# Attention values from plain fp32 weights, two key tiles in the two column halves of the PE array

## The chip, the cores and the metric

The kernel runs on one core of a Trainium2 chip. The metric is the device time of one execution in microseconds (us). The core has a tensor engine (PE, with its weight loads listed apart as PEld), a vector engine (DVE), a scalar engine (ACT), GpSimd (POOL) and a queue engine (SP) that starts most transfers. They run at the same time and wait for each other through semaphores. The kernel uses eight PSUM banks of 128 x 512 fp32 (tags mm 3, z 2, av, tr and hg 1 each).

## The reference

One layer of a decoder over 2048 tokens of width 1024: an input projection, two head groups side by side (an HGRN2 recurrence with 4 heads, a stick-breaking attention with 8 heads of width 64), an output projection, a dense SwiGLU feed-forward block and a gated per-layer embedding. The change lies in the attention:

```python
z = jnp.einsum('bthd,bshd->bhts', qb, kp).astype(jnp.float32) * scale
causal = jnp.arange(t1)[None, :] < jnp.arange(t0, t1)[:, None]
log_1mb = jnp.where(causal, -jax.nn.softplus(z), 0.0)
rem = lax.cumsum(log_1mb, axis=3, reverse=True) - log_1mb
a = jnp.where(causal, jnp.exp(jax.nn.log_sigmoid(z) + rem), 0.0)
outs.append(jnp.einsum('bhts,bshd->bthd', a.astype(v.dtype), vp))
```

For each query t the weight of key s is a sigmoid times the product of (1 - sigmoid) over the keys between them, and the last line sums the values with these weights. Everything is fp32.

## The kernel before

**Precision.** fp32 operands of the large products are split: `hi` is the value cast to the type fp32r, `lo` is what the cast left out, also in fp32r. A product is then the sum of two or three fp32r matmuls into one PSUM bank (`mm3`, lines 221 to 223: hi.hi, lo.hi, hi.lo). The HGRN group uses plain fp32 matmuls instead, some of them into a part of the array's columns (lines 503 and 514).

**Tiling of the attention.** The tokens are cut into four groups g of 512. For each query group, head and key group c up to g there is a chunk: 512 queries against 512 keys, 80 chunks in all, 32 of them on the diagonal (c = g). A chunk has four units, 320 in all. In the first half of a unit (`weights_of`) PE computes the scores of 128 queries against the chunk's keys into a bank "z" (line 388), ACT takes two sigmoids, DVE runs the product along the keys (line 409) and POOL multiplies to the weights `a`, 128 queries x 512 keys (line 413). Values need the keys on the partitions, so in `turn_of` PE transposes the `a` of all four query tiles for one key tile of 128 (line 421) into the one bank "tr". On the diagonal, key tile sb needs only the query tiles from sb on: 512, 384, 256 and 128 columns. ACT casts the turned weights to `ah` (line 424), DVE subtracts to `al` (line 426), and one unit later `values_of` adds two fp32r matmuls to the bank "av" (lines 437 and 438).

**The values.** The eviction of the v projection (`evict`, lines 323 to 332) writes each head's 64 columns twice, high part and rest side by side, 128 columns to DRAM (`v_s`). So the stationary tile `vt` of a unit is 128 keys x 128, and rows 0 to 63 of "av" gather the high part's sums, rows 64 to 127 the rest's. At the end of a head ACT copies the lower rows and DVE adds the two halves (lines 442 and 443).

**Order.** PE's order is the program's. The attention is a generator that yields twice per unit: after `weights_of` of unit i, and after `values_of` of an older unit followed by `turn_of` of unit i - 4 (LAG = 4). `weave` spreads these steps between the steps of the main stream: the input projections of the four groups first, then the output projections of groups 0 to 2, with the HGRN generators between them. Then follow the feed-forward block and the embedding, without attention. A scheduler orders the other engines' queues, each of which runs in order. The buffers around the change: one bank "tr", one bank "av", two each of `ah`, `al`, `kt` and `vt`, eight of `a`.

Of the kernel before, what the change touches and what calls it, by code (L numbers as in the profile page):

```python
# [8 lines left out]
F32 = mybir.dt.float32  # L9
F32R = mybir.dt.float32r  # L10
# [3 lines left out]
ALU = mybir.AluOpType  # L14

P = 128
# [3 lines left out]
GT = 512  # L20
NG = T // GT
TT = GT // P
HH = 4
SBH = 8
SBD = 64
# [59 lines left out]
def hybrid_block(  # L85
# [6 lines left out]
    nc = tc.nc  # L92
    ctx.enter_context(tc.manual_schedule(engines={mybir.EngineType.PE}))
    x, p, out = x[0], p[0, 0], out[0]
# [6 lines left out]
    def scratch(name, shape):  # L101
        return [dram.tile(list(shape), F32, tag=f"{name}{g}", name=f"{name}{g}") for g in range(NG)]

    q_s = scratch("q_s", (2, SBH, SBD, GT))
    k_s = scratch("k_s", (SBH, 2, SBD, GT))
    v_s = scratch("v_s", (GT, SBH, P))
    hq_s = scratch("hq_s", (HH, P, GT))
    hf_s = scratch("hf_s", (HH, P, GT))
    hv_s = scratch("hv_s", (GT, HH * P))
# [75 lines left out]
    def ev(dt=F32, name="ev", shape=(P, GT)):  # L185
        return fb.tile(list(shape), dt, tag="ev", name=name, bufs=12)
# [5 lines left out]
    att = side.enter_context(tc.tile_pool(name="att", bufs=2, side="right"))  # L192
# [35 lines left out]
    def dense(nk, w_in_cols, act, w_stationary):  # L228

        banks = [mm_bank() for _ in range(2)]  # L230
        for kk in range(0, nk, 2):
            w = weight(w_in_cols(kk))
            for i in range(2):
                for k in range(2):
                    a = act[kk + k]
                    first, last = kk + k == 0, kk + k == nk - 1
                    if w_stationary:
                        o = k * 256 + i * P
                        mm3(banks[i], [t[:, o:o + P] for t in w], a, first, last)
                    else:  # L240
                        mv = [t[:, k * 256:(k + 1) * 256] for t in w]
                        for j in range(2):
                            mm3(banks[i][:, j * 256:(j + 1) * 256], cut(a, 2 * i + j), mv, first and j == 0, last and j == 1)
                if i == 0 or kk < nk - 2:
                    yield None
        yield banks
# [58 lines left out]
    def in_proj(g, u, kinds):  # L305
        def cols(c):
            return lambda k: w_in[k * P:(k + 2) * P, c:c + 256]

        def evict(kind, half, i, b):
            j = 2 * half + i  # L310
            if kind in ("q", "k"):
                hi, lo = ev(F32R, "ea"), ev(F32R, "eb")
                nc.scalar.copy(hi, b)
                nc.vector.tensor_tensor(lo, b, hi.bitcast(F32), op=ALU.subtract)
                for n, s in enumerate((hi, lo)):
                    if kind == "q":
                        d = q_s[g][n, 2 * j:2 * j + 2]
                    else:
                        d = k_s[g][2 * j:2 * j + 2, n]
                    for hh in range(2):  # L320
                        nc.sync.dma_start(d[hh], s[hh * SBD:(hh + 1) * SBD, :].bitcast(F32))
            elif kind == "v":
                for n in range(2):
                    t = 2 * i + n
                    vv = ev(F32R, "vv").rearrange("p (h i d) -> p h i d", h=SBH // 2, i=2)
                    b3 = b[:, n * 256:(n + 1) * 256].rearrange("p (h d) -> p h d", d=SBD)
                    nc.scalar.copy(vv[:, :, 0, :], b3)
                    nc.vector.tensor_tensor(
                        vv[:, :, 1, :], b3, vv[:, :, 0, :].bitcast(F32), op=ALU.subtract)
                    nc.sync.dma_start(  # L330
                        v_s[g][t * P:(t + 1) * P, half * SBH // 2:(half + 1) * SBH // 2],
                        vv.rearrange("p h i d -> p h (i d)").bitcast(F32))
            elif kind == "hq":
                sg, e = ev(), ev()
                nc.scalar.activation(sg, b, AF.Sigmoid)
                nc.vector.tensor_tensor(e, b, sg, op=ALU.mult)
                nc.sync.dma_start(hq_s[g][j], e)
            elif kind == "hf":
                e = ev()
                nc.scalar.copy(e, b)  # L340
                nc.sync.dma_start(hf_s[g][j], e)
            elif kind == "hv":
                e = ev()
                nc.scalar.copy(e, b)
                d = hv_s[g][2 * i * P:2 * (i + 1) * P, half * 256:(half + 1) * 256]
                nc.sync.dma_start(d.rearrange("(t p) d -> p t d", p=P), e.rearrange("p (t d) -> p t d", t=2))
            else:
                sg, e = ev(), ev()
                nc.scalar.activation(sg, b, AF.Sigmoid)
                nc.vector.scalar_tensor_tensor(e, b, g_hg[:, j:j + 1], sg, op0=ALU.mult, op1=ALU.mult)  # L350
                nc.sync.dma_start(hg_s[g][j], e)

        for kind, c in kinds:
            for half in range(2):
                for banks in dense(ND, cols(c * 512 + half * 256), u, kind not in ("v", "hv")):
                    if banks is None:
                        yield
                for i, b in enumerate(banks):
                    evict(kind, half, i, b)
                yield  # L360


    def attention():
# [10 lines left out]
        def chunk_start(st, c):  # L374
            h = st["h"]
            kt = att.tile([P, GT], F32R, tag="kt", name="kt", bufs=2)
            nc.sync.dma_start(kt.bitcast(F32), k_s[c][h].rearrange("i d t -> (i d) t"))
            vt = att.tile([P, TT, P], F32R, tag="vt", name="vt", bufs=2)
            nc.sync.dma_start(vt.bitcast(F32), v_s[c][:, h, :].rearrange("(b s) d -> s b d", s=P))
            return {"st": st, "c": c, "k": kt, "v": vt, "a": []}  # L380

        def weights_of(ch, tb):
# [33 lines left out]
        def turn_of(ch, sb):  # L416
            diag = ch["c"] == ch["st"]["g"]
            t0 = sb if diag else 0
            tr = bank("tr")
            for tb in range(t0, TT):  # L420
                nc.tensor.transpose(tr[:, tb * P:(tb + 1) * P], ch["a"][tb][:, sb * P:(sb + 1) * P], ident)  # L421
            lo_c = t0 * P
            hi = att.tile([P, GT], F32R, tag="ah", name="ah")
            nc.scalar.copy(hi[:, lo_c:], tr[:, lo_c:])  # L424
            lo = att.tile([P, GT], F32R, tag="al", name="al")
            nc.vector.tensor_tensor(lo[:, lo_c:], tr[:, lo_c:], hi[:, lo_c:].bitcast(F32), op=ALU.subtract)  # L426
            return ch, sb, lo_c, hi, lo

        def values_of(ch, sb, lo_c, hi, lo):
            st, c = ch["st"], ch["c"]  # L430
            g = st["g"]
            first = c == g and sb == 0
            last = c == 0 and sb == TT - 1
            if first:
                st["av"] = bank("av")
            av = st["av"]
            nc.tensor.matmul(av[:, lo_c:], ch["v"][:, sb, :], hi[:, lo_c:], start=first, stop=False)
            nc.tensor.matmul(av[:, lo_c:], ch["v"][:, sb, :], lo[:, lo_c:], start=False, stop=last)
            if last:
                h = st["h"]  # L440
                o = att.tile([SBD, GT], F32, tag="avo", name="avo", bufs=1)
                nc.scalar.copy(o, av[SBD:P, :])
                nc.vector.tensor_tensor(o, av[0:SBD, :], o, op=ALU.add)
                nc.sync.dma_start(o_s[g][HH + h // 2][(h % 2) * SBD:(h % 2 + 1) * SBD, :], o)

        units, turned = [], []
        chunks = [(g, h, c) for g in range(NG) for h in range(SBH) for c in range(g, -1, -1)]
        n_units = len(chunks) * TT
        for i in range(n_units + LAG + 1):
            if i < n_units:  # L450
                if i % TT == 0:
                    g, h, c = chunks[i // TT]
                    if c == g:
                        st = head_start(g, h)
                    ch = chunk_start(st, c)
                weights_of(ch, i % TT)
                units.append((ch, i % TT))
            yield
            if turned:
                values_of(*turned.pop(0))  # L460
            if i >= LAG and i - LAG < n_units:
                turned.append(turn_of(*units[i - LAG]))
            yield

    LAG = 4

    def attention_steps(g):
        return SBH * (g + 1) * TT
# [657 lines left out]
    units = [attention_steps(g) for g in range(NG)]  # L1126
# [33 lines left out]
    turned = []  # L1160
# [5 lines left out]
    for g in range(NG - 1):  # L1166
        if g + 1 < NG - 1:
            out_load(g + 1, res[g + 1])
        op = Stream(out_proj(g, res[g]))
# [29 lines left out]
    op = Stream(out_proj(NG - 1, res[NG - 1]))  # L1199
# [73 lines left out]
```

## Time and profile before

| | |
|---|---|
| median of three runs | 3137.61 us (3127.91 to 3139.72) |
| the profiled execution's own time | 3140.98 us |
| its span, first to last instruction | 3139.2 us |
| mean granted TensorE clock | 0.971 |
| DVE, scan of the attention (line 409, 320 instructions) | 245.9 + 105.1 us |
| ACT, cast of the turned weights (line 424, 320 instructions) | 167.3 us, 523 ns each |
| POOL, the weights a (line 413, 320 instructions) | 314.0 us |

How to read the rows: a row of instructions has the line, the engine, the operation, out<-in, the shape, the count, the busy time with the mean of one in ns, and the idle time of that engine just before them with what ended it. A row of waits has who waited, for whom, the total in us, the times and the longest. A row of stretches has the window, its length, the busy time of each engine with its count, the granted clock and the share and rate of the transfers. A row of the timeline has the start, the length, the engine, the line, the operation and the count of merged instructions. Matmuls overlap, so what one costs is the time from its start to the next one's start.

### The profile page before, as it was taken

To read this page: it belongs to the slowest core of one execution; us is meant where nothing else is said; L and a number is where in the kernel's file an instruction comes from. 1 tells how busy PE (TensorE), PEld (TensorE's weight loads), DVE (VectorE), ACT (ScalarE), POOL (GpSimd) and SP (SyncE) were. 2 spreads that over 40 slices of the span, in tenths; PEclk is the share of its full clock that TensorE was granted. 3 is DMA by queue.
4 is the path that set the end of the run, shared out by engine and by line. 5 is a ranking of instruction groups with operands and counts; after the bars stand their busy time and mean duration, and the time that the engine had idled before them with its cause. 6 is when DMAs were issued, how large, how long until landed. Compare 5 with 4: busy or idle time off the path is not lost. (4 is left out here: it accounts for less than half of the span.)

```text
span 3139.2 us, 52948 instructions
## 1 busy us (share of the span) xinstructions
PE 2927.5 (93%) x18280; PEld 2455.3 (78%) x18280; DVE 2030.1 (65%) x2793; ACT 1587.0 (51%) x3187; POOL 1622.3 (52%) x1606
## 2 busy tenths in 40 slices
PE   7999899989999989778889999999999999998979
PEld 6888688868887878767767887888788888887757
DVE  3556566657677666654686677756786676746474
ACT  5666556656666666656543332355433333545432
POOL 3344355535556555755664444455744343657364
PEclk9999899989999999899999999999999999999989
DMA  6775465446445444546766676777855664678774
GB/s 189 224 212 163 128 182 162 146 134 174 150 142 156 145 138 118 182 134 228 239 219 208 228 246 220 225 230 221 290 185 186 204 217 132 220 221 278 253 258 148
DMA packets 463822, 607.02 MB, mean 193 GB/s; under 512 B 43456, under 2 KB 269760, under 8 KB 463552
## 3 DMA queue, kind: packets, MB, share of 16 engines
q1 hardware_dynamic: 463552, 603.63, 61.1%
q8 instruction: 144, 2.36, 0.3%
q14 instruction: 126, 1.03, 0.1%
HBM read 444.61 MB, written 158.86 MB: 192 GB/s over the span
## 5 line engine op out<-in xcount | busy, mean ns | idle before, releaser
L754 ACT CAST wh<-wr 128x512 fp32r<-128x512 f32 x600 | 354.1, 618 | 544.1 <-PE mm L222 165.6
L413 POOL TENSOR_TENSOR a<-be,ring 128x512 f32<-128x512 f32 (+2 forms) x320 | 314.0, 981 | 497.8 <-DVE ring L409 473.5
L755 POOL TENSOR_TENSOR wl<-wr,wh 128x512 fp32r<-128x512 f32 x256 | 370.4, 1454 | 360.9 <-ACT wh L754 343.6
L221 PE MATMUL mm<-uh,wh 128*128 128x512 f32 x1168 | 485.5, 416 | 4.4 <-DVE c L762 2.7
L223 PE MATMUL mm<-uh,wl 128*128 128x512 f32 x1168 | 461.8, 395 | 1.6 <-POOL wl L755 1.6
L222 PE MATMUL mm<-ul,wh 128*128 128x512 f32 x1168 | 461.2, 395 | 0.0
L755 DVE TENSOR_TENSOR wl<-wr,wh 128x512 fp32r<-128x512 f32 x344 | 313.0, 915 | 178.9 <-ACT wh L754 163.0
L221 PE MATMUL mm<-wh,uh 128*128 128x256 f32 (+1 forms) x1024 | 323.3, 316 | 9.0 <-ACT mix L643 6.4
L409 DVE TENSOR_TENSOR_SCAN ring<-z,ring,be 128x512 f32<-128x512 f32 x192 | 245.9, 1281 | 100.6 <-ACT z L395 96.9
L222 PE MATMUL mm<-wl,uh 128*128 128x256 f32 (+1 forms) x1024 | 306.7, 299 | 1.7 <-POOL wl L755 1.7
L223 PE MATMUL mm<-wh,ul 128*128 128x256 f32 (+1 forms) x1024 | 305.8, 299 | 0.0
L426 DVE TENSOR_TENSOR al<-tr,ah 128x512 fp32r<-128x512 f32 (+1 forms) x320 | 192.4, 601 | 113.3 <-ACT ah L424 112.6
L223 PEld LDWEIGHTS mm<-uh,wl 128*128 128x128 f32 x1168 | 222.2, 190 | 51.7 <-POOL wl L755 2.0
L221 PEld LDWEIGHTS mm<-uh,wh 128*128 128x128 f32 x1168 | 223.4, 191 | 46.9 <-DVE c L762 3.6
L207 ACT CAST wh<-wr 128x512 fp32r<-128x512 f32 x288 | 177.9, 618 | 151.9 <-PE mm L222 79.2
L222 PEld LDWEIGHTS mm<-ul,wh 128*128 128x128 f32 x1168 | 223.2, 191 | 38.6
L208 POOL TENSOR_TENSOR wl<-wr,wh 128x512 fp32r<-128x512 f32 x144 | 187.5, 1302 | 84.1 <-ACT wh L207 78.9
L394 ACT ACTIVATE be<-z 128x512 f32<-128x512 f32 (+2 forms) x320 | 170.9, 534 | 103.2 <-PE z L388 50.3
L221 PEld LDWEIGHTS mm<-wh,uh 128*128 128x128 f32 x1024 | 201.9, 197 | 17.8 <-ACT mix L643 7.2
L424 ACT CAST ah<-tr 128x512 fp32r<-128x512 f32 (+1 forms) x320 | 167.3, 523 | 95.6 <-PE tr L421 91.4
L222 PEld LDWEIGHTS mm<-wl,uh 128*128 128x128 f32 x1024 | 202.4, 198 | 7.3 <-POOL wl L755 2.0
L223 PEld LDWEIGHTS mm<-wh,ul 128*128 128x128 f32 x1024 | 201.9, 197 | 3.9
(287 smaller groups left out, 7256.5 us busy)
## 6 DMA issues: line engine op xcount, KB each, us to landing
wr<-in_w_gate_up_dram SPq DMA_DIRECT2D x308, 256.0 KB, 3.9
wr<-in_w_in_dram SPq DMA_DIRECT2D x224, 256.0 KB, 3.3
wr<-hid_s SPq DMA_DIRECT2D x154, 256.0 KB, 3.0
wr<-in_w_down_dram SPq DMA_DIRECT2D x110, 256.0 KB, 3.4
wr<-h_s SPq DMA_DIRECT2D x96, 256.0 KB, 4.3
hid_s<-hs SPq DMA_DIRECT2D x88, 256.0 KB, 3.1
wr<-wd_s SPq DMA_DIRECT2D x88, 256.0 KB, 3.5
kt<-k_s SPq DMA_DIRECT2D x80, 256.0 KB, 3.0
```

Source lines behind the costliest of these rows:

```text
L207: nc.scalar.copy(hi, src)
L208: (lo_engine or nc.gpsimd).tensor_tensor(lo, src, hi.bitcast(F32), op=ALU.subtract)
L221: nc.tensor.matmul(o, l[0], r[0], start=start, stop=False)
L222: nc.tensor.matmul(o, l[0], r[1], start=False, stop=False)
L223: nc.tensor.matmul(o, l[1], r[0], start=False, stop=stop)
L394: nc.scalar.activation(be[:, :n], z[:, :n], AF.Sigmoid, scale=0.125)
L409: nc.vector.tensor_tensor_scan(r[:, o:o + n][:, ::-1], z[:, :n][:, ::-1], be[:, :n][:, ::-1], init, op0=ALU.mult, op1=ALU.bypass)
L413: nc.gpsimd.tensor_tensor(a[:, :n], be[:, :n], r[:, o + 1:o + n + 1], op=ALU.mult)
L424: nc.scalar.copy(hi[:, lo_c:], tr[:, lo_c:])
L426: nc.vector.tensor_tensor(lo[:, lo_c:], tr[:, lo_c:], hi[:, lo_c:].bitcast(F32), op=ALU.subtract)
L754: nc.scalar.copy(hi, src)
L755: lo_engine.tensor_tensor(lo, src, hi.bitcast(F32), op=ALU.subtract)
```

## The change

One unit's values become one plain fp32 matmul. `v_s` holds each head's 64 columns once, and its eviction is one copy. `turn_of` makes one fp32 tile `at` by ACT's copy; DVE takes no part. `values_of` now runs once for two units: key tiles sb0 and sb0 + 1 each get one matmul with 64 stationary columns, the first into rows 0 to 63 of "av", the second into rows 64 to 127, that is, into the two column halves of the array. The sum of the two halves at the end of a head stays as it was. Since the first pair of a head has to start both halves on all 512 columns, key tile 1 of a diagonal chunk is filled up with zeros on its first 128 columns (POOL) and its matmul takes 512 columns instead of 384. `at` has three buffers. A pair runs in the second half of the step after its second tile was turned, so the first tile of a pair is used two units behind its turn, the second one unit.

```diff
-    v_s = scratch("v_s", (GT, SBH, P))
+    v_s = scratch("v_s", (GT, SBH, SBD))
...
-                    vv = ev(F32R, "vv").rearrange("p (h i d) -> p h i d", h=SBH // 2, i=2)
-                    b3 = b[:, n * 256:(n + 1) * 256].rearrange("p (h d) -> p h d", d=SBD)
-                    nc.scalar.copy(vv[:, :, 0, :], b3)
-                    nc.vector.tensor_tensor(
-                        vv[:, :, 1, :], b3, vv[:, :, 0, :].bitcast(F32), op=ALU.subtract)
+                    vv = ev(name="vv")[:, 0:256]
+                    nc.scalar.copy(vv, b[:, n * 256:(n + 1) * 256])
...
-            vt = att.tile([P, TT, P], F32R, tag="vt", name="vt", bufs=2)
-            nc.sync.dma_start(vt.bitcast(F32), v_s[c][:, h, :].rearrange("(b s) d -> s b d", s=P))
+            vt = att.tile([P, TT, SBD], F32, tag="vt", name="vt", bufs=2)
+            nc.sync.dma_start(vt, v_s[c][:, h, :].rearrange("(b s) d -> s b d", s=P))
...
-            hi = att.tile([P, GT], F32R, tag="ah", name="ah")
-            nc.scalar.copy(hi[:, lo_c:], tr[:, lo_c:])
-            lo = att.tile([P, GT], F32R, tag="al", name="al")
-            nc.vector.tensor_tensor(lo[:, lo_c:], tr[:, lo_c:], hi[:, lo_c:].bitcast(F32), op=ALU.subtract)
-            return ch, sb, lo_c, hi, lo
+            at = att.tile([P, GT], F32, tag="at", name="at", bufs=3)
+            nc.scalar.copy(at[:, lo_c:], tr[:, lo_c:])
+            if t0 == 1:
+                nc.gpsimd.memset(at[:, 0:lo_c], 0.0)
+                lo_c = 0
+            return lo_c, at
...
-            nc.tensor.matmul(av[:, lo_c:], ch["v"][:, sb, :], hi[:, lo_c:], start=first, stop=False)
-            nc.tensor.matmul(av[:, lo_c:], ch["v"][:, sb, :], lo[:, lo_c:], start=False, stop=last)
+            for i, (lo_c, at) in enumerate(pair):
+                nc.tensor.matmul(
+                    av[i * SBD:(i + 1) * SBD, lo_c:], ch["v"][:, sb0 + i, :], at[:, lo_c:], start=first, stop=last)
...
-            if turned:
-                values_of(*turned.pop(0))
+            if len(pair) == 2:
+                values_of(*units[i - LAG - 2], pair)
+                pair = []
             if i >= LAG and i - LAG < n_units:
-                turned.append(turn_of(*units[i - LAG]))
+                pair.append(turn_of(*units[i - LAG]))
```

Line numbers of the changed kernel are shifted by up to three: its scores stand on line 385, its transposes on 418, its copy on 421, its fill on 423 and its value matmuls on 437.

PE in the input projection of a later group, before: each unit has its two value matmuls ahead of its transposes.

```order
L437 MATMUL av<-ah,vt 128x512
L438 MATMUL av<-al,vt 128x512
L421 MATMUL tr<-ident,a 128x128 x3
L514 MATMUL hg<-qp,ks 32x32 x8
L221 MATMUL mm<-wh,uh 128x256
L222 MATMUL mm<-wl,uh 128x256
```

PE in the changed kernel, at a like place; the second transposes belong to the next unit.

```order
L437 MATMUL av<-at,vt 64x512 x2
L418 MATMUL tr<-ident,a 128x128 x4
L385 MATMUL z<-kt,q_9497 128x512
L385 MATMUL z<-kt,q_9500 128x512
L221 MATMUL mm<-uh,wh 128x512
L222 MATMUL mm<-ul,wh 128x512
L223 MATMUL mm<-uh,wl 128x512
L221 MATMUL mm<-uh,wh 128x512
L222 MATMUL mm<-ul,wh 128x512
L223 MATMUL mm<-uh,wl 128x512
L418 MATMUL tr<-ident,a 128x128 x3
```

Every second unit now has two narrow matmuls ahead of its transposes, and the other has none.

DVE in the first units of group 1, before (ring is the scan's output, ev and wl are other work of DVE):

```order
L336 TENSOR_TENSOR ev<-mm,ev 128x512
L409 SCALAR_TENSOR_TENSOR ring_251<-z,be 128x128
L426 TENSOR_TENSOR al<-tr,ah 128x512
L409 SCALAR_TENSOR_TENSOR ring_253<-z,be 128x256
L426 TENSOR_TENSOR al<-tr,ah 128x512
L409 SCALAR_TENSOR_TENSOR ring_255<-z,be 128x384
L208 TENSOR_TENSOR wl<-wr,wh 128x512
L426 TENSOR_TENSOR al<-tr,ah 128x512
L409 SCALAR_TENSOR_TENSOR ring_257<-z,be 128x512
L426 TENSOR_TENSOR al<-tr,ah 128x512
L409 SCALAR_TENSOR_TENSOR ring_251<-z,ring_251,be 128x512
L336 TENSOR_TENSOR ev<-mm,ev 128x512
```

The same place in the changed kernel:

```order
L333 TENSOR_TENSOR ev<-mm,ev 128x512
L406 SCALAR_TENSOR_TENSOR ring_251<-z,be 128x128
L406 SCALAR_TENSOR_TENSOR ring_253<-z,be 128x256
L406 SCALAR_TENSOR_TENSOR ring_255<-z,be 128x384
L208 TENSOR_TENSOR wl<-wr,wh 128x512
L406 SCALAR_TENSOR_TENSOR ring_257<-z,be 128x512
L406 SCALAR_TENSOR_TENSOR ring_251<-z,ring_251,be 128x512
L333 TENSOR_TENSOR ev<-mm,ev 128x512
```

The subtractions are gone, and the rest stands in the same order. On POOL each diagonal chunk has a fill between two products, here in group 0 of the changed kernel:

```order
L410 TENSOR_TENSOR a<-be,ring_257 128x512
L423 MEMSET at 128x128
L410 TENSOR_TENSOR a<-be,ring_251 128x128
L410 TENSOR_TENSOR a<-be,ring_253 128x256
L208 TENSOR_TENSOR wl<-wr,wh 128x512
```

Before, the rows there were the same without the fill.

More of the change, by code (lines that the diff above doesn't have):

```diff
@@ L324, in evict @@
                     t = 2 * i + n
-                    vv = ev(F32R, "vv").rearrange("p (h i d) -> p h i d", h=SBH // 2, i=2)
-                    b3 = b[:, n * 256:(n + 1) * 256].rearrange("p (h d) -> p h d", d=SBD)
-                    nc.scalar.copy(vv[:, :, 0, :], b3)
-                    nc.vector.tensor_tensor(
-                        vv[:, :, 1, :], b3, vv[:, :, 0, :].bitcast(F32), op=ALU.subtract)
+                    vv = ev(name="vv")[:, 0:256]
+                    nc.scalar.copy(vv, b[:, n * 256:(n + 1) * 256])
                     nc.sync.dma_start(
                         v_s[g][t * P:(t + 1) * P, half * SBH // 2:(half + 1) * SBH // 2],
-                        vv.rearrange("p h i d -> p h (i d)").bitcast(F32))
+                        vv.rearrange("p (h d) -> p h d", d=SBD))
             elif kind == "hq":
@@ L422, in turn_of, with values_of @@
             lo_c = t0 * P
-            hi = att.tile([P, GT], F32R, tag="ah", name="ah")
-            nc.scalar.copy(hi[:, lo_c:], tr[:, lo_c:])
-            lo = att.tile([P, GT], F32R, tag="al", name="al")
-            nc.vector.tensor_tensor(lo[:, lo_c:], tr[:, lo_c:], hi[:, lo_c:].bitcast(F32), op=ALU.subtract)
-            return ch, sb, lo_c, hi, lo
-        def values_of(ch, sb, lo_c, hi, lo):
+            at = att.tile([P, GT], F32, tag="at", name="at", bufs=3)
[4 more added lines that the diff above has]
+            return lo_c, at
+        def values_of(ch, sb0, pair):
             st, c = ch["st"], ch["c"]
             g = st["g"]
-            first = c == g and sb == 0
-            last = c == 0 and sb == TT - 1
+            first = c == g and sb0 == 0
+            last = c == 0 and sb0 == TT - 2
             if first:
@@ L444, in values_of @@
                 nc.sync.dma_start(o_s[g][HH + h // 2][(h % 2) * SBD:(h % 2 + 1) * SBD, :], o)
-        units, turned = [], []
+        units, pair = [], []
         chunks = [(g, h, c) for g in range(NG) for h in range(SBH) for c in range(g, -1, -1)]
```

## The prediction

> **What bounds the kernel now.** I read the page's engine line first, then the table of stretches, then PE's waits, and last the timeline of PE around single blocks.
>
> ```profile
> PE 2927.5 (93%) x18280; PEld 2455.3 (78%) x18280; DVE 2030.1 (65%) x2793; ACT 1587.0 (51%) x3187; POOL 1622.3 (52%) x1606
> 200.00:400.00 200.00, 17.25 (x48) 9.26 (x48) 0.96 0.53 157
> ...
> 1000.00:1200.00 200.00, 17.95 (x47) 8.88 (x46) 0.97 0.45 134
> 1200.00:1400.00 200.00, 13.65 (x34) 6.92 (x34) 0.94 0.48 150
> 1400.00:1600.00 200.00, 3.87 (x9) 1.86 (x9) 0.90 0.66 221
> ```
> The first row is the page's; the others are the stretches of the high value matmul alone (line 437: PE busy and count, weight-load busy and count, granted clock, DMA). The attention runs from about 100 to 1600 us and ends thinly: of 320 units only 34 + 9 stand behind 1200 us. Behind 1600 us nothing of the change runs.
>
> ```profile
> 400.00:600.00 200.00, 199.53 (x1787) 169.43 (x1786) 133.40 (x197) 125.38 (x268) 106.84 (x136) 1.00 0.55 163
> ...
> 1200.00:1400.00 200.00, 164.80 (x1749) 147.86 (x1747) 118.44 (x180) 124.66 (x274) 123.17 (x160) 0.94 0.48 150
> 1400.00:1600.00 200.00, 157.70 (x1211) 144.70 (x1211) 129.22 (x171) 117.17 (x253) 126.06 (x136) 0.90 0.66 221
> ```
> The same table for all engines (PE, PEld, DVE, ACT, POOL, clock). Up to about 1100 us PE is nearly full and its clock whole: there PE time is run time. From 1200 to 1600 PE idles 35 and 42 us per 200 and waits for others. So the change has two scales: what it does to PE's own time, and which waits it takes away.
>
> **PE's own time for the values.** A normal unit, and the short blocks of the diagonal, from the timeline (start, length, engine, line):
>
> ```profile
> 419.10 0.39 PE L437 MATMUL av<-ah,vt 128*128 128x512 f32 x1
> 419.33 0.39 PE L438 MATMUL av<-al,vt 128*128 128x512 f32 x1
> 419.56 0.60 PE L421 MATMUL tr<-ident,a 128*128 128x128 f32 x4
> ...
> 500.50 0.33 PE L437 MATMUL av<-ah,vt 128*128 128x384 f32 x1
> 500.67 0.34 PE L438 MATMUL av<-al,vt 128*128 128x384 f32 x1
> 500.85 0.38 PE L421 MATMUL tr<-ident,a 128*128 128x128 f32 x2
> ```
> ```profile
> 396.78 0.27 PE L437 MATMUL av<-ah,vt 128*128 128x256 f32 x1
> 396.90 0.28 PE L438 MATMUL av<-al,vt 128*128 128x256 f32 x1
> 397.01 0.27 PE L421 MATMUL tr<-ident,a 128*128 128x128 f32 x1
> ...
> 400.72 0.22 PE L437 MATMUL av<-ah,vt 128*128 128x128 f32 x1
> 400.78 0.28 PE L438 MATMUL av<-al,vt 128*128 128x128 f32 x1
> 400.89 0.62 PE L421 MATMUL tr<-ident,a 128*128 128x128 f32 x4
> ```
> What counts is start to start, since lengths overlap: 0.23 us for a 512-column fp32r matmul, so 0.46 for a unit, 0.35 at 384 columns, 0.23 at 256, 0.17 at 128. Two units, the size of the new pair, take 0.92 us off the diagonal, 0.81 for the diagonal's first two and 0.40 for its last two.
>
> After the change a unit is one plain fp32 matmul. The HGRN group has such matmuls, one of them into 64 columns of the array, another into 32:
>
> ```profile
> 421.38 0.38 PE L567 MATMUL hg<-score,v 128*128 128x128 f32 x2
> 421.60 0.39 PE L568 MATMUL hg<-qp,hstate 128*128 128x128 f32 x2
> ...
> 462.05 0.63 PE L388 MATMUL z<-kt,q 128*128 128x512 f32 x2
> 462.61 0.68 PE L514 MATMUL hg<-qp,ks 128*64 128x64 f32 x8
> 463.22 0.39 PE L221 MATMUL mm<-wh,uh 128*128 128x256 f32 x1
> 463.44 0.29 PE L222 MATMUL mm<-wl,uh 128*128 128x256 f32 x1
> 463.56 0.28 PE L223 MATMUL mm<-wh,ul 128*128 128x256 f32 x1
> ```
> Line 567 is one matmul of the code and two instructions in the record: 0.22 us for 128 columns, 0.11 per instruction. By proportion a 512-column fp32 matmul is two instructions of 0.44 us, against 2 x 0.23 for the two fp32r ones. Alone it would take 0.88 us; only if the two column halves stream at once does a pair cost 0.88 and not 1.76.
>
> Do they? Line 503 puts 16 matmuls of 32 columns into the four column strips in turn:
>
> ```profile
> 680.13 0.46 PE L503 MATMUL hg<-qp,ks 128*32 128x32 f32 x32
> 680.52 0.50 PE L221 MATMUL mm<-uh,wh 128*128 128x512 f32 x1
> ```
> A 32-column instruction is a quarter of 0.11, 0.0275 us; one after another, 32 of them would take 0.88 us. They take 0.39, entry and exit included. Four abreast would be 8 x 0.0275 = 0.22, and the 0.17 left is just the entry and exit of line 514 below. So strips run side by side, in fp32 too. No row shows it for two halves of 512 columns; the ends are 0.88 and 1.76 us per pair, and I take 0.88, by this nearest row.
>
> The price of narrow work is in the 64-column rows. From the two score matmuls at 462.05 to line 514 pass 0.56 us, where two such take 0.46 (419.10 to 419.56): 0.10 lost at the entry. The eight instructions take 0.61 where 8 x 0.055 is 0.44: 0.17 for a weight load that nothing covers and for running empty. The next full matmul takes 0.22 where its neighbour takes 0.12: 0.10, its weight load uncovered. Together 0.37 us per narrow block, and the new order makes one of each pair, 160 in all.
>
> The Trainium skill, in "TensorEngine Tiling (Array Packing)", Key Properties, says that "Changing tiling mode (not just tile) drains the TensorE", with no size. The trace agrees and sizes it at 0.37 us; without that drain the PE term below would be about nothing, so the rule speaks against this change.
>
> Pairs: 1.25 us each (0.44 + 0.44 + 0.37); the diagonal's last pair 0.22 + 0.22 + 0.37 = 0.81. The 96 pairs off the diagonal gain 0.33 each, 32 us; the 32 first pairs of the diagonal, whose second tile is filled up with zeros to 512 columns, 0.44, 14 us; the 32 last pairs 0.41, 13 us. Sum 59 us. The proportion counts an instruction's fixed part four times over, so I take **+55 us**. The exposed weight load falls on the transposes behind the pair instead of line 221; they load a tile each too, so I price it alike.
>
> **Waits that go.** The value matmuls wait for the split today:
>
> ```profile
> L437 PEld LDWEIGHTS av<-ah,vt 128*128 128x128 f32 x320 | 62.1, 194 | 16.0 <-ACT ah L424 8.6
> L438 PEld LDWEIGHTS av<-al,vt 128*128 128x128 f32 x320 | 61.4, 192 | 24.5 <-DVE al L426 17.6
> L426 DVE TENSOR_TENSOR al<-tr,ah 128x512 fp32r<-128x512 f32 (+1 forms) x320 | 192.4, 601 | 113.3 <-ACT ah L424 112.6
> ```
> Weight loads idle 8.6 + 17.6 = 26 us for it. In the new order a tile is evicted by ACT alone and used one or two units later, so this goes: **-24 us** (least 13, PE's own idle at the two lines; most 26). PE's waits from 200 to 1750 us:
>
> ```profile
> PE tr L294 <- DVE ul L297: 14.9, 8, 2.8
> ...
> PE tr L688 <- DVE al L426: 10.3, 6, 2.3
> PE tr L294 <- DVE al L426: 8.3, 5, 2.4
> ...
> PE av L438 <- DVE al L426: 7.1, 11, 1.1
> PE hg L503 <- DVE ks L542: 7.0, 3, 4.3
> ...
> PE av L437 <- ACT ah L424: 5.8, 6, 3.0
> ```
> The one "tr" bank is freed by DVE's subtraction today, by ACT's copy afterwards. The 18.6 us of waits for "al" at lines 688 and 294 shrink by a 0.60 us subtraction and its place in DVE's queue, 11 times; they can't vanish, for the copy comes late too. Bounds 0 and -18.6; I take half, **-9 us**. Other waits name DVE operations that stood behind the subtraction: "ul" and "ks" here, 22 us, and about as much again in smaller rows. The subtraction holds DVE for 192 us and blocks its queue for 113 more while it waits, a fifth of the 1500 us; I take a fifth of 44, **-9 us**, bounds 0 and -44. Behind 1200 us 21 pairs run where PE waits for others anyway; half of their 7 us is hidden, **-4 us**.
>
> Costed at nothing: ACT's copy (same 320, same size) and 32 fills of 128 columns on POOL, 52% busy. A fill waits for a value pair on PE and stands ahead of the next "a" products in POOL's queue, but those are needed four units later; were that cover gone, PE would wait at the transposes, where "a" costs it 2.7 us in all today. Reading and writing half the bytes of v saves 15 of 607 MB of transfers that PE hardly waits for, in pieces half as long. The removed subtraction at the v eviction (32 times 415 ns) is in DVE's fifth.
>
> ```profile
> L421 PE MATMUL tr<-ident,a 128*128 128x128 f32 x1088 | 176.1, 277 | 8.5 <-DVE rg L634 4.9 <-POOL a L413 2.7 <-DVE ul L297 0.9
> L328 DVE TENSOR_TENSOR vv<-mm,vv 128x256 fp32r<-128x256 f32 x32 | 13.1, 415 | 11.1 <-ACT vv L327 10.8
> ```
> **Sum.** 55 - 24 - 9 - 9 - 4 = +9 us on the profiled execution's 3141.0, so 3150. That execution lies 3.4 us above the median of the runs, 3137.6, so I forecast 3147 for a median: slightly slower, within the 0.5% (16 us) that a measurement of this kernel can tell from no change.
>
> **Rivals.**
> *The passes go strictly in order.* If each fp32 matmul's two instructions stand together and PE keeps their order, the two of the first half run one after the other, and only the second of them overlaps the first of the other half: three times 0.44 instead of two. Price 128 x 0.44 + 32 x 0.22 = 63 us, so 3147 + 63 = 3210. It decides from the first pair in the stretch up to 1100 us, where PE has no slack. Against it: line 503 would need 17 x 0.0275 = 0.47 us without entry and exit, and takes 0.39 with them. For it: that row has 32 columns, not 512. Chance 0.11. The Trainium skill, "TensorE: Matmul & The Clock Gate", Part 3: Packing small matmuls, states such an order: matmuls start and end in program order, a strict FIFO without reordering.
> *The halves don't overlap at all*, so the change doesn't do what it says: twice that price, 127 us, 3274. Line 503 speaks against it twice as strongly. Chance 0.07.
> *DVE was the hidden brake.* All named waits go at their full bounds: 55 - 26 - 19 - 44 - 7 = -41, so 3097. For it: DVE's queue is blocked 113 us by one line and PE idles most from 1200 to 1600 us, where these waits lie. Against it: there POOL and ACT are named as often, and the stretches up to 1100 us have no slack to give back. Chance 0.14.
>
> **How the numbers follow.** The forecast has 0.68, with a range of its own from 3115 to 3175 (the bounds of the waits, not all at one end). For 8 in 10 the range goes down to most of the DVE case and up past the forecast's end towards the in-order case: 3105 to 3195. Faster by over 0.5% (below 3122): most of the DVE case and a sliver of the forecast, 0.16. Slower by over 0.5% (above 3153): 0.18 from the two PE rivals and a third of the forecast, 0.40. Within: 0.44.
>
> **What would show it.** In the new profile's timeline a pair of 512 columns should take some 1.05 us from its first start to the first transpose (in order 1.5, one by one 1.9), with 0.33 instead of 0.23 us from the matmul before it. The waits for "ah" and "al" should be gone from the value lines, and lines 294 and 688 should name ACT. From 400 to 1100 us the work should take longer, from 1200 to 1600 us PE should idle less. I am wrong if 512-column halves don't overlap, or if the waits behind DVE vanish altogether.

## The result and the profile after

The changed kernel takes 3157.16 us (median of 5 runs, 3153.83 to 3161.15) against 3137.61 for the kernel before (5 runs, 3127.68 to 3139.72): a ratio of 1.0073, with a 95% interval of 1.0051 to 1.0095. Taken again, on the chip of e1, e6 and e8 below, it gave 1.0066 (1.0051 to 1.0082). So the change costs about 20 to 23 us. The two profiled executions differ by less, 3152.1 against 3139.2 us of span; the one of before was longer than any of these five runs.

First the engine line of the page after, and the stretches of all engines as quoted before (PE, PEld, DVE, ACT, POOL, clock, transfers):

```profile
PE 2952.7 (94%) x18280; PEld 2366.3 (75%) x18280; DVE 1862.8 (59%) x2441; ACT 1586.8 (50%) x3187; POOL 1633.9 (52%) x1638
```
```profile
400.00:600.00 200.00, 200.00 (x1748) 152.46 (x1742) 102.39 (x137) 120.78 (x259) 106.16 (x138) 1.00 0.52 148
...
1200.00:1400.00 200.00, 168.34 (x1718) 139.90 (x1717) 102.29 (x150) 122.89 (x271) 123.18 (x161) 0.92 0.44 138
1400.00:1600.00 200.00, 165.13 (x1315) 150.12 (x1313) 112.21 (x147) 114.49 (x245) 126.96 (x137) 0.91 0.66 216
```
DVE does 167 us less, ACT what it did, POOL 12 us more. PE is full to the last tenth from 400 to 600 us and got fewer matmuls through (1748 for 1787). From 1200 to 1600 it idles 67 us where it idled 77.

The timeline of PE around a pair of 512 columns, and around the diagonal's last pair (256 and 128 columns); start, length, line:

```profile
410.12 0.40 PE L223 MATMUL mm<-uh,wl 128*128 128x512 f32 x1
410.45 1.08 PE L437 MATMUL av<-at,vt 128*64 128x512 f32 x4
411.46 0.66 PE L418 MATMUL tr<-ident,a 128*128 128x128 f32 x4
411.87 0.48 PE L221 MATMUL mm<-uh,wh 128*128 128x512 f32 x1
```
```profile
441.17 0.40 PE L223 MATMUL mm<-uh,wl 128*128 128x512 f32 x1
441.50 0.65 PE L437 MATMUL av<-at,vt 128*64 128x256 f32 x4
442.08 0.66 PE L418 MATMUL tr<-ident,a 128*128 128x128 f32 x4
```
The pair is four instructions in the record. From its start to the first transpose pass 1.01 us; four instructions of 0.44 us, the prediction's estimate, would need 1.76 one after the other. So the halves stream side by side; e1_same_half below tests it. Ahead of the pair pass 0.33 us instead of 0.23, and the four transposes behind it take 0.41 where they took 0.35 (419.56 to 419.91 before). A pair costs 0.10 + 1.01 + 0.06 = 1.17 us, the small one 0.10 + 0.58 + 0.06 = 0.74.

PE's waits from 200 to 1750 us, those rows that answer to the ones quoted before:

```profile
PE tr L294 <- DVE ul L297: 17.2, 8, 3.1
PE hg L504 <- DVE ks L543: 15.1, 5, 5.1
...
PE av L223 <- DVE wl L756: 8.1, 2, 5.7
...
PE tr L689 <- ACT at L421: 4.9, 6, 1.4
...
PE tr L418 <- ACT at L421: 3.2, 4, 1.6
...
PE tr L294 <- ACT at L421: 2.5, 4, 1.3
...
PE av L437 <- ACT at L421: 0.2, 1, 0.2
```
The value matmuls wait for nothing any more (0.2 us). The tr bank is now waited for through ACT, 10.6 us where "al" alone cost 18.6. But the waits for other work of DVE did not shrink although DVE lost a twelfth of its work: "ul" went from 14.9 to 17.2, "ks" from 7.0 to 15.1. Some smaller rows fell; all rows that name DVE for anything but "al" add up to 46.5 us before, 51.7 after, and 49.5 in the changed kernel's second trace.

Where in the program is the time lost? Each HGRN generator ends with the same matmul (line 582, after the change 583), so its starts are marks. The timeline rows before, and after:

```profile
641.51 0.95 PE L582 MATMUL hg<-ones,acc 128*128 128x1 f32 x8
...
951.67 0.50 PE L582 MATMUL hg<-ones,acc 128*128 128x1 f32 x4
...
1203.44 0.73 PE L582 MATMUL hg<-ones,acc 128*128 128x1 f32 x6
...
1452.54 0.95 PE L582 MATMUL hg<-ones,acc 128*128 128x1 f32 x8
```
```profile
648.04 0.95 PE L583 MATMUL hg<-ones,acc 128*128 128x1 f32 x8
...
960.97 0.72 PE L583 MATMUL hg<-ones,acc 128*128 128x1 f32 x6
...
1214.89 0.84 PE L583 MATMUL hg<-ones,acc 128*128 128x1 f32 x7
...
1466.97 1.05 PE L583 MATMUL hg<-ones,acc 128*128 128x1 f32 x8
```
The changed kernel is 6.5, 9.3, 11.5 and 14.4 us late at the four marks: the loss grows with the attention, most steeply at its beginning. The last mark lies just behind the last value matmul, so I call the time up to it the attention part; single traces repeat it well (the changed kernel's second one has this mark at 1467.5).

To see which work holds PE longer, I summed in the traces, up to that mark, the time from each matmul's start to the next one's, by what the first of the two does (us; the other columns are experiments below):

```
                  before  after  e2     e5     e4     e1     e8
dense products     803.9  812.2  816.5  804.1  809.5  806.5  800.5
HGRN               147.7  151.0  147.4  146.1  148.3  143.7  142.1
other transposes    42.4   49.7   46.1   41.9   47.6   44.5   43.4
scores             158.5  157.9  164.2  156.7  154.1  156.5  190.5
transposes of a    126.7  127.9  132.7  126.8  121.9  123.3  124.9
values             156.5  151.7  155.7  157.0  138.0  268.4  152.4
sum               1435.7 1450.3 1462.7 1432.7 1419.4 1542.9 1453.8
```
At the undisturbed spacings quoted in the prediction, the values before would have needed 96 x 0.92 + 32 x 0.81 + 32 x 0.40 = 127 us. They held PE for 156.5, 30 us more. After, 128 x 1.01 + 32 x 0.58 = 148 of 151.7 are the pairs themselves.

Not all of the 30 us is waiting for the split. If each spacing is compared with the median of the same two instructions, about 15 us stand ahead of the second value matmul, 6 at the transposes behind it, and 7 lie where PE had half its clock. Another 7 us stand ahead of the first value matmul, in the rows of what runs before it. So the value lines waited some 22 us.

The half clock is a term of its own. Of the attention's stretches, before and then after, these two gained most clock, the third number from the end:

```profile
200.00:400.00 200.00, 183.42 (x1183) 151.94 (x1182) 115.33 (x160) 122.20 (x255) 85.54 (x96) 0.96 0.53 157
...
600.00:800.00 200.00, 187.83 (x1452) 156.30 (x1451) 133.81 (x191) 123.38 (x264) 97.02 (x129) 0.96 0.52 152
```
```profile
200.00:400.00 200.00, 187.36 (x1213) 138.91 (x1209) 89.85 (x106) 124.61 (x260) 88.27 (x104) 0.99 0.50 148
...
600.00:800.00 200.00, 188.84 (x1474) 139.62 (x1473) 104.95 (x137) 124.37 (x266) 96.95 (x127) 0.99 0.48 139
```
The traces' clock records are either 1.00 or 0.50. In a stretch at 0.50 the dense matmuls start 0.43 us apart instead of 0.23, here before the change, just behind two waits of PE:

```profile
338.82 0.63 PE L223 MATMUL mm<-uh,wl 128*128 128x512 f32 x1
339.25 0.63 PE L221 MATMUL mm<-uh,wh 128*128 128x512 f32 x1
```
Up to the last mark 82 us lie at half the clock before, and 58 us in both traces of the changed kernel. I estimate the gain from it at 11 us by the spacings, at most 12, half of the difference. What sets the clock was not tried.

### The profile page after: what moved, and what is told of

Same layout as the page of the kernel before. It is cut to its first block, busy times and chain, and to the rows that moved or that the text cites. A ratio compares the mean times of both kernels' runs of the same rounds, so it can differ in the third digit from the quotient of the medians.

```text
span 3152.1 us, 52361 instructions
## 1 busy us (share of the span) xinstructions
PE 2952.7 (94%) x18280; PEld 2366.3 (75%) x18280; DVE 1862.8 (59%) x2441; ACT 1586.8 (50%) x3187; POOL 1633.9 (52%) x1638
## 5 line engine op out<-in xcount | busy, mean ns | idle before, releaser
L756 DVE TENSOR_TENSOR wl<-wr,wh 128x512 fp32r<-128x512 f32 x344 | 311.5, 912 | 169.7 <-ACT wh L755 155.0
L418 PEld LDWEIGHTS tr<-ident,a 128*128 128x128 f32 x1088 | 122.8, 141 | 139.6 <-issue 107.0
L421 ACT COPY at<-tr 128x512 f32<-128x512 f32 (+1 forms) x320 | 167.2, 522 | 112.8 <-PE tr L418 111.0
L208 DVE TENSOR_TENSOR wl<-wr,wh 128x512 fp32r<-128x512 f32 x144 | 122.9, 853 | 167.0 <-ACT wh L207 96.6
```

The source lines that it names most:

```text
L208: (lo_engine or nc.gpsimd).tensor_tensor(lo, src, hi.bitcast(F32), op=ALU.subtract)
L421: nc.scalar.copy(at[:, lo_c:], tr[:, lo_c:])
L756: lo_engine.tensor_tensor(lo, src, hi.bitcast(F32), op=ALU.subtract)
```

## The experiments

All ratios are to the kernel before on the same chip, and I turn them into us by its 3136. Eight kernels ran.

**e1_same_half: do the halves run at the same time?** Both matmuls of a pair go to rows 0 to 63, and the end of a head copies these rows without an addition.

```diff
-                    av[i * SBD:(i + 1) * SBD, lo_c:], ch["v"][:, sb0 + i, :], at[:, lo_c:], start=first, stop=last)
+                    av[0:SBD, lo_c:], ch["v"][:, sb0 + i, :], at[:, lo_c:], start=first and i == 0, stop=last and i == 1)
...
-                nc.scalar.copy(o, av[SBD:P, :])
-                nc.vector.tensor_tensor(o, av[0:SBD, :], o, op=ALU.add)
+                nc.scalar.copy(o, av[0:SBD, :])
```

> The changed kernel with both matmuls of a pair in the lower column half, rows 0 to 63 of av, one after the other; the end of a head copies that half and adds nothing. Same instructions on PE, no overlap possible. Theory A (the halves stream side by side in the changed kernel, as its trace shows them 7 ns apart): 128 pairs lose 0.86 us and 32 lose 0.22, 117 us, less what of it hides waits: 3260 to 3275. Rival (the two starts 7 ns apart are only how the record shows them, and the halves share the array one after the other): 3157.

Measured: 3247.35 us (4 runs), ratio 1.0363 (1.0342 to 1.0384), 114 us above before and 91 to 93 above the changed kernel; that is below the 3260 to 3275 expected, and nowhere near the rival's 3157. Its timeline has the pair, and its marks:

```profile
433.15 0.40 PE L223 MATMUL mm<-uh,wl 128*128 128x512 f32 x1
433.48 1.93 PE L437 MATMUL av<-at,vt 128*64 128x512 f32 x4
435.34 0.44 PE L418 MATMUL tr<-ident,a 128*128 128x128 f32 x2
```
```profile
691.30 0.84 PE L582 MATMUL hg<-ones,acc 128*128 128x1 f32 x7
...
1037.81 0.83 PE L582 MATMUL hg<-ones,acc 128*128 128x1 f32 x7
...
1309.60 0.62 PE L582 MATMUL hg<-ones,acc 128*128 128x1 f32 x5
...
1561.11 1.05 PE L582 MATMUL hg<-ones,acc 128*128 128x1 f32 x8
```
The same four instructions take 1.86 us where they took 1.01: in the changed kernel the halves do overlap, and fully. The values hold PE 268.4 - 151.7 = 117 us longer, as reckoned, but the time grows by 92. The marks show where the other 25 went: against the changed kernel this one is 43, 77, 95 and 94 us late. Up to the second mark the added PE time is paid in full (by then 83 pairs of 512 columns and 26 small ones have run: 83 x 0.86 + 26 x 0.22 = 77); between the third and the fourth nothing is, where PE waits for others anyway. Less of this trace lies at half the clock, too: 44 us up to the last mark, against 58.

**e4_four and e6_split: fewer and more borders.** The first runs the two pairs of a chunk as one narrow block, with five buffers of `at` instead of three; the second cuts 72 pairs into two blocks of 256 columns, one ahead of the transposes and one behind them.

```diff
-            if len(pair) == 2:
-                values_of(*units[i - LAG - 2], pair)
+            if len(pair) == TT:
+                for n in (0, 2):
+                    values_of(*units[i - LAG - TT + n], pair[n:n + 2])
```

> The changed kernel with the two pairs of a chunk back to back, so 80 narrow blocks instead of 160; nothing else of the work changes (five at buffers). The trace of the changed kernel has 0.30 us per narrow block beside the streaming: 0.10 at the entry, 0.15 inside, 0.06 at the transpose behind it. Theory A (entering and leaving narrow work is what the change pays): 80 x 0.30 = 24 us less, 3133. Rival (the price lies in streaming fp32, the blocks' borders are hidden elsewhere): 3157.

```diff
+            old, pair = (pair, []) if len(pair) == 2 else (None, pair)
+            if old:
+                values_of(*units[i - LAG - 2], old, 0)
             if i >= LAG and i - LAG < n_units:
                 pair.append(turn_of(*units[i - LAG]))
+            if old:
+                values_of(*units[i - LAG - 2], old, 1)
...
+                if first or last:
+                    c0, c1 = lo_c, GT if part == 0 else 0
+                else:
+                    c0, c1 = max(lo_c, part * GT // 2), (part + 1) * GT // 2
```

> The changed kernel with 72 of its 160 pairs cut into two narrow blocks of 256 columns, one ahead of the transposes and one behind them: the same columns streamed, 232 narrow blocks instead of 160 (the first and last pair of a head stay whole). With e4_four it halves and raises the number of borders. Theory A (0.30 us per narrow block on the path): 72 x 0.30 = 22 us more than the changed kernel, 3180. Rival (the gain of e4_four came from something else than fewer borders, such as later use of the tiles): 3157.

Measured: e4_four 3128.33 us (11 runs), ratio 0.9978 (0.9965 to 0.9990), 28 to 30 us below the changed kernel where 24 were expected, and a little faster than the kernel before. e6_split 3178.50 us (4 runs), ratio 1.0139 (1.0122 to 1.0156), 21 to 23 us above the changed kernel where 22 were expected. The timeline of e4_four has the block of a chunk:

```profile
411.97 0.39 PE L223 MATMUL mm<-uh,wl 128*128 128x512 f32 x1
412.29 1.94 PE L437 MATMUL av<-at,vt 128*64 128x512 f32 x8
414.16 0.66 PE L418 MATMUL tr<-ident,a 128*128 128x128 f32 x4
```
Two pairs in one block take 1.87 us, 0.15 less than twice 1.01; with one entry (0.10) and one late transpose (0.06) saved that makes 0.31 for a border. So borders are on the path and cost 0.3 us each: fewer of them shorten the time by what they cost and more of them lengthen it. By these numbers a fp32 pair without its border would hold PE for 0.86 us, the split matmuls of two units 0.92. e4_four uses its tiles later as well, but the value matmuls of the changed kernel had only 0.2 us of named waits left to lose.

**e2_subtract_bank and e3_subtract_only: DVE's work back, without its result.** One line in each, behind ACT's copy:

```diff
+            nc.vector.tensor_tensor(lo[:, lo_c:], tr[:, lo_c:], at[:, lo_c:], op=ALU.subtract)
```
```diff
+            nc.vector.tensor_tensor(lo[:, lo_c:], at[:, lo_c:], at[:, lo_c:], op=ALU.subtract)
```

> The changed kernel with DVE's subtraction of the turned weights put back as idle work: it reads the tr bank and at, and nobody reads what it writes. So DVE is loaded as before and the tr bank is freed by DVE as before, but the value matmuls don't wait for it. Theory A (the prediction's two terms of 9 us: DVE's relief gives back time through the tr bank and through its queue): 18 us above the changed kernel, about 3175. Theory B (all that was given back comes from the value matmuls no longer waiting): as the changed kernel, 3157.

> As e2_subtract_bank, but the idle subtraction reads at alone, so the tr bank is freed by ACT and only DVE's queue is loaded. Theory A (9 us by the queue, 9 by the bank): 3166, halfway between the changed kernel and e2. If the bank has no share: as e2. If the queue has none: 3157.

Measured: e2 3168.22 us (5 runs), ratio 1.0102 (1.0086 to 1.0118), 10 us above the changed kernel's 1.007, halfway between the theories. e3 3165.08 us (6 runs), ratio 1.0087 (1.0073 to 1.0102), 5 us above by the ratios and 8 to 10 by the medians; its interval overlaps both. In e3 the subtraction took 846 ns on average over its four widths instead of 601, so it loads DVE more than before and doesn't separate queue from bank. PE's waits in e2:

```profile
PE tr L294 <- DVE ul L297: 15.4, 8, 2.8
PE hg L506 <- DVE ks L545: 14.9, 5, 5.1
PE tr L691 <- DVE al L423: 11.1, 6, 3.0
...
PE tr L418 <- DVE al L423: 8.1, 9, 2.0
```
"al" holds the tr bank again, but "ul" and "ks" cost what they cost in the changed kernel, with or without the subtraction in DVE's queue; all rows for DVE's other work are 43.0 us from 200 to 1750, no more than the 51.7 without it. In the table e2 stands 12 us above the changed kernel: 15 in the scores, the transposes of a and the values, 4 in the dense products, and 7 less in the rest. So having DVE's work back costs some 10 us; how it parts into bank and queue isn't settled. In e3's trace, the longest of its six runs, the attention part is 15 us above the changed kernel although ACT frees the bank. The clock has a share in both: 75 us of e2 and 85 of e3 lie at half of it, against 58, which is worth at most 9 and 14 us.

**e5_late: the split kernel with a unit more of time.** The kernel before; its value matmuls run two units behind the turn instead of one.

```diff
-            if turned:
+            if len(turned) == 2 or turned and i == n_units + LAG + 1:
                 values_of(*turned.pop(0))
```

> The kernel before with its two fp32r value matmuls one unit later, so that the split has a whole unit more; same work, same buffers. Theory A (the changed kernel's gain was the wait of the value matmuls for the split, and lateness alone would have brought it): 20 us below before, 3117. Rival (the wait only moves to the next thing that PE waits for): 3137.

Measured: 3126.92 us (7 runs), ratio 0.9964 (0.9950 to 0.9979): 11 us less than before, about half of what was expected, and the fastest kernel of the study with e4_four. The trace doesn't bear the theory out. PE's waits:

```profile
PE tr L294 <- DVE ul L297: 14.9, 8, 2.8
PE tr L421 <- DVE al L426: 14.1, 11, 4.1
...
PE tr L688 <- DVE al L426: 10.9, 6, 2.3
PE tr L294 <- DVE al L426: 8.3, 5, 2.3
```
The value lines no longer wait for "al", but the transposes behind them now do, 14.1 us at line 421 where there was no such wait: the subtraction also frees the one tr bank. In the table the values hold PE for 157.0 us as before, since a wait at the transposes falls behind the last value matmul. The attention part is 3 us shorter in its one trace. The other 8 us lie behind it, where the edit has nothing; why, stays open.

**e8_late_busy: is added PE time hidden?** e5_late with 33 us of PE work added.

```diff
             z = bank("z")
+            if tb % 2:
+                nc.tensor.matmul(z[:, :n], st["q"][0][:, tb * P:(tb + 1) * P], ch["k"][:, :n], start=True, stop=True)
```

> e5_late with PE time added to it: the first score matmul of every second unit runs twice (160 more, 33 us in all by 0.23 us for 512 columns), nothing else. Question: why did the changed kernel get more back than the runs with DVE's relief and with lateness account for (46 us of PE time added, 20 us paid, 10 from DVE, 8 from lateness)? Theory A (added PE time gives ACT and DVE time to catch up, so that a part of it hides waits for the tr bank and others): a third of the 33 us hidden, about 3149. Rival (PE time is paid in full): 3127 + 33 = 3160.

Measured: 3155.28 us (6 runs), ratio 1.0066 (1.0052 to 1.0081), 32 us above e5_late by the ratios and 28 by the medians: paid nearly in full, so the timed runs don't bear out a third. The single traces have 21 us in the attention part, less than the 32 of the scores' row, which would fit a third; and 65 us at half the clock where e5_late has 82. As e5_late gained 8 us in its trace where its edit has nothing, the question stays open.

**e7_again** is the changed kernel on the chip of e1, e6 and e8: 3155.18 us (6 runs), the ratio given above.

> The changed kernel itself once more, on the same chip as the other three, for comparison: 3157 by both theories.

## Why the prediction was right, and where its terms were off

The forecast was 3147, slightly slower; measured were 3157, in the range and on the forecast side, though beyond the 0.5% that it was put within: +20 us instead of +9. By its steps:

- **The halves stream at once (0.88 us per pair).** Right: 1.01 us from the pair's start to the first transpose where 1.05 was forecast, and 1.86 when they share a half. The row of 32-column strips carried over to 512 columns. The four instructions of a pair start at 0, 7, 480 and 487 ns in the trace, in twos. Both PE rivals, the order of passes (1.5 us) and no overlap (1.9 us), are out by the same rows.
- **The border (0.37 us).** The mechanism right, the size 0.3: the entry 0.10 as forecast, the inside 0.15 instead of 0.17, and 0.06 instead of 0.10 behind. That last part was priced by a 256-column matmul; why it is less at the transposes was not tried.
- **PE's own time (+55 us).** With 1.17 and 0.74 us it is 96 x 0.25 + 32 x 0.36 + 32 x 0.34 = +46.
- **The waits of the value lines (-24 us).** They went, to 0.2 us of named waits, and by the spacings some 22 us had stood there. But e5_late shows that later use alone doesn't bring it: in the old order "al" gates the tr bank next. In e2_subtract_bank, with the later use but DVE on the bank, 8.1 us of waits for "al" stand at the transposes. So both count; their shares were not separated.
- **The tr bank (-9 us).** The named waits fell from 18.6 to 10.6 us. (The 0.60 us of the subtraction is a mean over four widths; at 512 columns it took 0.68.) e2_subtract_bank, which gives the bank and the load back to DVE, costs 10.
- **DVE's queue (-9 us).** This step failed. I took a fifth off the waits for "ul", "ks" and the like, because the subtraction held a fifth of DVE's time. All rows that name DVE's other work went from 46.5 to 51.7 us instead. With the subtraction back they are 43.0 in e2 and 59.2 in e3, so the sum moves by more than the term for other reasons, and less load on DVE shrank nothing that can be told. What these waits hang on was not tried.
- **Hidden behind 1200 us (-4 us).** The place was right: e1_same_half pays all of its added PE time up to the second mark and none behind the third. The size for this change can't be told from the runs.
- **Not in the sum: the clock.** I called it whole up to about 1100 us, though the rows of before have 0.96 in two of these stretches, and counted nothing for it. 24 us less at half the clock are worth some 11 us.

So 46 - 22 - 11 = 13 us stands against 14 measured in the attention part: the terms of 9, 9 and 4 came to nearly nothing together. It is luck that the clock, which I had not counted, made up for half of them. From 14 us in the traces to 22 in the timed runs is within what single executions of the kernel before differ by (3128 to 3145).

The rival of a hidden brake on DVE, at 3097, is out: the kernel became slower, and with all of the subtraction away the waits for DVE's other work did not fall. That PE has no slack up to 1100 us was too coarse: it was nearly full by the busy digits, and yet some 13 of the 22 us that the value lines waited lie there. The idle columns named 13 of the 22 us in all: PE's records overlap (0.39 us long, 0.23 apart), so a matmul can start late without PE being idle.

## What to carry to other kernels

Two plain fp32 matmuls of 64 columns ran beside each other in different column halves (1.01 us for a pair, 1.86 in one half), so count such a pair by one; then add the price of each change between full and narrow work, 0.3 us here, and put narrow work into as few blocks as the buffers allow. What an engine no longer does is worth what PE waited for its results, not the engine's busy time: DVE was 167 us less busy, and little came back by it beyond the 22 us that PE had waited at the value lines; another 11 us came with the clock. And a wait that is moved off one line can go to the next user of the same buffer, as in e5_late, unless that is freed earlier as well.

## What the runs showed of the hardware that was not expected

A 128 x 512 subtraction on DVE with fp32r output took 682 ns with one operand in PSUM (e2) and 913 ns with both reads from SBUF (e3), in the same place of the same kernel. POOL's products for `a` (line 410) took 985 ns on average in e2 and 1085 in e3. Why was not tried. The rows of e2 and e3:

```profile
L423 DVE TENSOR_TENSOR al<-tr,at 128x512 fp32r<-128x512 f32 x224 | 152.9, 682 | 104.3 <-ACT at L421 103.6
```
```profile
L423 DVE TENSOR_TENSOR al<-at 128x512 fp32r<-128x512 f32 x224 | 204.5, 913 | 100.1 <-ACT at L421 99.5
```
